# RWKV steps in the order of a list schedule, and experts with eleven weight pieces split ahead and one pinned, in a hybrid layer on one Trainium2 core

## The chip, the cores and the metric

The kernel runs on one core of a Trainium2 chip. The metric is device time in microseconds. Three runs of the kernel before gave 3416.99, 3421.06 and 3427.79 us (median 3421.06). Engines: PE (matmuls), DVE (vector), ACT (scalar), POOL (GpSimd) and SP, which here only issues transfers. Each engine takes its instructions in order; semaphores order the engines against each other.

## The reference, cut to what matters

One layer over 256 context and 2048 latent tokens of width 1024: modulation, one input projection, an mLSTM group and an RWKV-7 group of 8 heads each (64 wide, both scanned forwards and backwards), an output projection with layer norm, then a mixture of 32 SwiGLU experts (two per token) and a last layer norm. What the change touches:

```python
def step(state, inp):                       # RWKV, one token; scanned in two directions
    r_t, w_t, k_t, v_t, kh_t, a_t = inp
    removed = jnp.einsum('zhvk,zhk->zhv', state, kh_t)
    state = (state * w_t[:, :, None, :] - removed[..., None] * (kh_t * a_t)[:, :, None, :]
             + v_t[..., None] * k_t[:, :, None, :])
    return state, jnp.einsum('zhvk,zhk->zhv', state, r_t)

def expert_block(args):                     # 128 tokens of one expert in this kernel
    idx, w, e = args
    xb = tok_pad[idx]
    hb = jax.nn.silu(xb @ ex_gate[e]) * (xb @ ex_up[e])
    return (hb @ ex_down[e]) * w[:, None]
```

## The kernel before, in words

**RWKV stage** (`rwkv`). The 2304 tokens are cut into 9 groups (n) of 256 tokens, a group into 4 chunks of 64 (cc = 2 c2 + c). Both directions (d) go side by side on the halves of the partitions. Per group there is

- *Build*, four times (c2, d). The constructor issues four `pk` loads on SP (L891, 320 KB each, into one of two buffers). `exps` makes decay factors on ACT (L907 to L909), `rows` four DVE products (L917 to L921) that fill KR and BK, `products` 16 small matmuls for each of two chunks (L931) into two PSUM tiles `rpg` and two DVE masks into GM (L935), `turn` a transpose on PE (L940) and a copy on ACT (L941). `rpg` has four buffers.
- *Solve*, once for the group: the 32x32 triangular blocks of GM go through DRAM into `sM` (eight stores `BL` on SP, L963, and two loads, L965), 31 pairs of DVE operations of growing and shrinking size solve them (`steps`, L973 and L975), and `back` brings them home: two stores `YD` (L983), a transposing copy on ACT (L980), two stores `TD` (L985), twelve loads into GM and `T1` (L991, L992). `join(c2)` makes 64x64 inverses out of the blocks: 32 matmuls (L1002), two ACT copies (L1008), 32 matmuls (L1014), two ACT copies (L1019). Its buffers exist once (`sM`, `sY`, `T1`).
- *Chain*, once per chunk, 36 in a row, each needing the state S of the one before: `keys` (PE: 32 matmuls with S, L1046, and 32, L1059; two ACT copies, L1062), `query` (32 matmuls, L1046, latent groups only), `inverse` (32 matmuls, L1071; two ACT copies, L1074), `update` (32 matmuls, L1081), `state` (two DVE operations, L1087 and L1089), `outputs` (32 matmuls, L1097; one ACT copy, L1100; two POOL stores). POOL loads its V rows ahead (L1036).

The order on PE, DVE, ACT and SP is the program's own (`manual_schedule`); POOL's is left to the framework. Before, it is written out by hand: eight Builds and the Solve of group 0 as a prologue, and then a loop over the 36 chunks that puts the Builds of the next two groups (`PLAN`) and pieces of the next group's 31 solve pairs (`CUT`: down to pairs 32, 27, 24 in the first chunk, 23, 17, 15 in the second, and so on) at fixed places between the parts of a Chain. A `state` comes on DVE behind the second piece of its chunk's pairs.

**Experts** (`moe`). The 32 experts follow one another. A weight piece (`split`) is an ACT cast to `eH` (L1531) and a DVE subtraction to `eL` (L1532) of 128x1024 elements; an expert has 12 (4 gate, 4 up, 4 down), in 13 buffers. Eight are split during the expert before (`AHEAD`), pieces 8 and 9 at the expert's start (L1706), and `gate_up` pins the last two with `more(2, m)` (L1609): on DVE they come behind `m`, the first half of the gated product (`mult(0)`, L1622), by an order edge that binds DVE alone; the framework's scheduler places the rest. Behind them on DVE come `aL` (L1553), the low part of the transposed product, and `mult(1)`. Then a branch (L1737) lets further blocks of 128 tokens in, and `tail` multiplies by the down pieces (`epo`, L1565).

Of the kernel before, what the change touches and what calls it, by code (L numbers as in the profile page):

```python
# [8 lines left out]
F = mybir.dt.float32  # L9
# [44 lines left out]
class Kern:  # L54
# [786 lines left out]
    def rwkv(self):  # L841
        tc, nc, s = self.tc, self.nc, self.scratch
        self.Y = s("Y", [2, SEQ, 512])
        with ExitStack() as es:
# [35 lines left out]
            class Build:  # L880
# [3 lines left out]
                def __init__(b, n, c2, d):  # L884
                    b.n, b.c2, b.d, b.g = n, c2, d, grp[d][n]
                    b.lat = b.g > 0
# [24 lines left out]
                def rows(b):  # L911
                    d, v, E, EI = b.d, b.v, Es[b.d], b.v["cu"]
                    b.KR = gp.tile([128, 2, 4, 128], F, name="KR%d" % d)
                    ko, ro = slice(KO[d], KO[d] + 64), slice(RO[d], RO[d] + 64)
# [3 lines left out]
                    nc.vector.tensor_tensor(put(b.BK, ko), b.scan(v["ba"]), b.scan(EI), op=OP.mult)  # L918
                    nc.vector.tensor_tensor(put(b.BK, ro), b.nat(v["km"]), b.nat(EI), op=OP.mult)
# [3 lines left out]
                def products(b, c):  # L923
# [4 lines left out]
                    pG = [pg.tile([128, 4, 128], F, name="rpg") for _ in range(2)]  # L928
                    for q in range(4):
                        for e in range(2):  # L930
                            nc.tensor.matmul(pG[e][:, q, b.cols], b.BK[HD[e], c, q, :], b.KR[HD[e], c, q, b.cols], start=True,  # L931
                                             stop=True, tile_position=(64 * e, 0))
                    m = mask[:, b.d, b.cols][:, None, :].to_broadcast([128, 4, b.cols.stop - b.cols.start])
                    for e in range(2):
                        nc.vector.tensor_tensor(b.GM[:, c, e::2, b.cols], pG[e][:, :, b.cols], m, op=OP.mult)  # L935

                def turn(b, c):
                    pT = pg.tile([128, 4, 128], F, name="rpg")
                    for q in range(4):
                        nc.tensor.transpose(pT[:, q, :], b.BK[:, c, q, :], self.ident)  # L940
                    nc.scalar.copy(b.BT[:, c], pT)  # L941
# [6 lines left out]
            class Solve:  # L948


                def __init__(z, n):
                    z.n, z.j = n, 31
                    z.M = sp.tile([128, 32, 32], F, name="sM")
# [4 lines left out]
                    BLs = [dp.tile([64, 32, 32], F, name="BL%d" % d) for d in range(2)]  # L958
                    for d in range(2):
                        for c2 in range(2):  # L960
                            for i in range(2):
                                b = blk(d, i)
                                nc.sync.dma_start(pr(BLs[d], i, c2), GMf(n, c2, d)[b, :, b])  # L963
                    for d in range(2):
                        nc.sync.dma_start(z.M[64 * d:64 * d + 64], BLs[d])  # L965
# [11 lines left out]
                def back(z):  # L977
                    n, Y = z.n, z.Y
                    YT = sp.tile([128, 32, 32], F, name="sYT")
                    nc.scalar.copy(YT, Y.rearrange("p s t -> p t s"))  # L980
                    YDs, TDs = ([dp.tile([64, 32, 32], F, name="%s%d" % (x, d)) for d in range(2)] for x in ("YD", "TD"))
                    for d in range(2):
                        nc.sync.dma_start(YDs[d], Y[64 * d:64 * d + 64])  # L983
                    for d in range(2):
                        nc.sync.dma_start(TDs[d], YT[64 * d:64 * d + 64])  # L985
# [8 lines left out]
                def join(z, c2):  # L994
                    n, T1 = z.n, z.T1
                    cs = slice(2 * c2, 2 * c2 + 2)
                    Q = pg.tile([128, 16, 32], F, name="rpg")
                    for c in range(2):
                        for h in range(8):
                            for d in range(2):  # L1000
                                lo, hi = blk(d, 0), blk(d, 1)
                                nc.tensor.matmul(Q[hi, 8 * c + h, :], G[n, c2, d][2][lo, c, h, hi], T1[lo, 2 * c2 + c, h, :],  # L1002
                                                 start=True, stop=True, tile_position=(lo.start, hi.start))
                    qs = []
                    for d in range(2):
                        hi = blk(d, 1)
                        qs.append(T1[hi, cs].rearrange("p c h t -> p (c h) t"))
                        nc.scalar.copy(qs[d], Q[hi])  # L1008
                    Q = pg.tile([128, 16, 32], F, name="rpg")
                    for c in range(2):  # L1010
                        for h in range(8):
                            for d in range(2):
                                lo, hi = blk(d, 0), blk(d, 1)
                                nc.tensor.matmul(Q[lo, 8 * c + h, :], qs[d][:, 8 * c + h, :], G[n, c2, d][2][hi, c, h, hi],  # L1014
                                                 start=True, stop=True, tile_position=(hi.start, lo.start))
                    for d in range(2):
                        lo, hi = blk(d, 0), blk(d, 1)
                        src = Q[lo].rearrange("p (c h) t -> p c h t", c=2)
                        nc.scalar.activation(G[n, c2, d][2][lo, :, :, hi], src, AF.Copy, scale=-1.0)  # L1019
# [3 lines left out]
            class Chain:  # L1023
# [31 lines left out]
                def keys(k):  # L1055
                    K = k.K
                    k.from_state(ZKv, K)
                    for q, e, d, h in k.heads():
                        nc.tensor.matmul(ZKv[K[d], e, q, :], k.W[d][2][:, k.c, h, K[d]], k.VZ[d][:, h, :], start=False, stop=False,  # L1059
                                         skip_group_check=True, tile_position=(0, KO[d]))  # L1060
                    for d in range(2):
                        nc.scalar.copy(hv(k.UV[d][K[d]]), ZKv[K[d]])  # L1062
# [5 lines left out]
                def inverse(k):  # L1068
                    K = k.K
                    for q, e, d, h in k.heads():  # L1070
                        nc.tensor.matmul(ZKv[K[d], e, q, :], k.W[d][2][K[d], k.c, h, K[d]], k.UV[d][K[d], h, :], start=True, stop=True,  # L1071
                                         skip_group_check=True, tile_position=(KO[d], KO[d]))
                    for d in range(2):
# [776 lines left out]
```

## Time and profile before

| | us |
|---|---|
| median of three runs (lowest to highest) | 3421.06 (3416.99 to 3427.79) |
| time of the profiled execution | 3418.58 |
| its span | 3417.0 |
| PE, DVE, ACT, POOL busy in the span | 2866.9, 2339.6, 1364.0, 879.0 |
| RWKV stage: first Build's exponentials to last state | 1248.0 to 1944.3 |
| of it, the 36 Chains | 1363.5 to 1944.3 |
| experts: first gate product to last down product | 2306.7 to 3351 |

Times in rows are us from the span's start. A timeline row reads: start, duration, engine, line, operation, out<-in, shape and count, and in brackets the engine's idle time just before it with what ended it. A wait row reads: engine and line that waited, on what; total us, times, longest. A row of the lines view reads: group, count | busy us in total, mean ns of one | idle before it. A windows row reads: stretch and its length; busy us of PE, PEld, DVE, ACT and POOL with their instructions; granted PE clock; share of the DMA engines in use; GB/s.

### The profile page before, as it was taken

How to read it: one execution, taken by the hardware profiler on the slowest of the kernel's cores; microseconds unless marked ns; L12 is line 12 of the kernel's file. 1: busy time of each engine (PE TensorE's matmuls, PEld its weight loads, DVE VectorE, ACT ScalarE, POOL GpSimd, SP SyncE). 2: the span in 40 equal slices, each digit the busy share in tenths (PEclk: the TensorE clock that was granted, in tenths of full speed). 3: DMA queues.
4: the chain of work that ended last, by engine and by line, in shares of the span. 5: the costliest groups of instructions: out<-in, count | busy, mean ns of one | idle time of the engine just before them, and what ended most of it. 6: DMA issues, size and time to landing. Idle time of an engine off the chain costs nothing. (4 is left out here: it accounts for less than half of the span.)

```text
span 3417.0 us, 61401 instructions
## 1 busy us (share of the span) xinstructions
PE 2866.9 (84%) x24042; PEld 2405.9 (70%) x24042; DVE 2339.6 (68%) x3822; ACT 1364.0 (40%) x2187; POOL 879.0 (26%) x862
## 2 busy tenths in 40 slices
PE   6899999999979964777777588859899989989992
PEld 3677788898757754666666567647778877878781
DVE  4488888766787875667656288875877736476447
ACT  4432322335545322334344233344655525355233
POOL 5400000013455660112112365431222212122210
PEclk9899999999979875778788789979999999999996
DMA  5333332235468534666664554448988848597535
GB/s 187 117 114 108 101 116 82 88 101 189 164 219 242 167 109 115 171 159 170 155 168 128 159 174 137 141 147 286 334 295 284 304 125 276 159 335 234 177 112 209
DMA packets 471689, 602.59 MB, mean 176 GB/s; under 512 B 127222, under 2 KB 312338, under 8 KB 471314
## 3 DMA queue, kind: packets, MB, share of 16 engines
q1 hardware_dynamic: 413617, 441.15, 41.2%
q0 software_dynamic: 36736, 129.33, 13.0%
q10 hardware_dynamic: 20960, 27.20, 2.5%
q8 instruction: 224, 3.67, 0.5%
q14 instruction: 152, 1.24, 0.1%
HBM read 453.24 MB, written 144.33 MB: 175 GB/s over the span
## 5 line engine op out<-in xcount | busy, mean ns | idle before, releaser
L1532 DVE TENSOR_TENSOR eL<-eraw,eH 128x1024 fp32r<-128x1024 f32 x384 | 449.6, 1221 | 28.6 <-ACT eH L1531 24.6
L329 DVE SCALAR_TENSOR_TENSOR cacc<-P,cw,cacc 128x1008 f32<-128x1008 f32 (+3 forms) x320 | 398.7, 1247 | 56.5 <-ACT cacc L304 45.6
L1531 ACT CAST eH<-eraw 128x1024 fp32r<-128x1024 f32 x384 | 370.9, 1052 | 48.3 <-PEq L1737 35.1
L263 PE MATMUL in_ps<-hH,w_H 128*128 128x512 f32 (+1 forms) x664 | 252.3, 382 | 1.7 <-ACT pl_ev L355 1.7
L263 PE MATMUL in_ps<-hL,w_H 128*128 128x512 f32 (+1 forms) x664 | 249.6, 377 | 0.0
L263 PE MATMUL in_ps<-hH,w_L 128*128 128x512 f32 (+1 forms) x664 | 248.0, 374 | 0.0
L1565 PE MATMUL epo<-eH,aH 128*128 128x512 f32 x408 | 172.2, 422 | 64.8 <-DVEq L1737 32.2
L1651 POOL DMA_INDIRECT ACC<-yo,ids x32 | 131.0, 4093 | 250.5 <-DVE yo L1650 226.1
L1565 PE MATMUL epo<-eH,aL 128*128 128x512 f32 x408 | 159.7, 404 | 11.7 <-DVE aL L1553 11.7
L1565 PE MATMUL epo<-eL,aH 128*128 128x512 f32 x408 | 163.2, 400 | 0.0
L931 PE MATMUL rpg<-KR,BK 64*128 64x128 f32 (+1 forms) x1152 | 122.4, 350 | 46.7 <-ACT BT L941 17.5
L237 POOL DMA_DIRECT2D w_raw<-in_w_in x28 | 21.2, 757 | 506.2 <-DVE w_L L251 371.8
L263 PEld LDWEIGHTS in_ps<-hH,w_H 128*128 128x128 f32 x664 | 126.2, 191 | 34.6 <-issue 11.5
L931 PEld LDWEIGHTS rpg<-KR,BK 64*128 64x128 f32 x1152 | 104.9, 248 | 63.2 <-issue 23.8
L973 DVE TENSOR_TENSOR sT<-sM,sY 128x31 f32<-128x31 f32 (+15 forms) x279 | 95.3, 342 | 78.8 <-DMA sM<-BL 70.8
L298 ACT COPY P<-in_ps 128x512 f32<-128x512 f32 (+1 forms) x92 | 51.3, 557 | 235.8 <-PE in_ps L263 235.8
L1565 PE MATMUL epu<-eH,xL 128*128 128x256 f32 x512 | 143.4, 283 | 0.0
L1565 PE MATMUL epu<-eL,xH 128*128 128x256 f32 x512 | 143.2, 283 | 0.0
L263 PEld LDWEIGHTS in_ps<-hL,w_H 128*128 128x128 f32 x664 | 126.2, 190 | 22.7 <-issue 2.1
L1565 PE MATMUL epu<-eH,xH 128*128 128x256 f32 x512 | 142.2, 288 | 0.0
L263 PEld LDWEIGHTS in_ps<-hH,w_L 128*128 128x128 f32 x664 | 126.1, 190 | 22.3 <-issue 0.8
L1565 PEld LDWEIGHTS epo<-eH,aH 128*128 128x128 f32 x408 | 78.9, 193 | 83.1 <-ACT xH L1548 30.7
(471 smaller groups left out, 8151.1 us busy)
## 6 DMA issues: line engine op xcount, KB each, us to landing
eraw<-in_ex_gate SPq DMA_DIRECT2D x64, 1024.0 KB
eraw<-in_ex_up SPq DMA_DIRECT2D x64, 1024.0 KB
eraw<-in_ex_down SPq DMA_DIRECT2D x64, 1024.0 KB
pk<-PK SPq DMA_DIRECT2D x144, 320.0 KB
PK<-pk POOLq DMA_DIRECT2D x36, 768.0 KB, 3.9
ada_w<-in_w_ada SPq DMA_DIRECT2D x32, 512.0 KB
v<-MV SPq DMA_DIRECT2D x50, 264.0 KB
kc<-KTd SPq DMA_DIRECT2D x50, 256.0 KB
```

Source lines behind the costliest of these rows:

```text
L237: self.wld = nc.gpsimd.dma_start(w[:, 4:8, o:o + cn], src[:, 4:8])
L263: nc.tensor.matmul(o, a[:, k, :], b, start=i == 0, stop=i == 3 * KT - 1)
L298: nc.scalar.copy(P[:, t0:t0 + n], ps)
L329: nc.vector.scalar_tensor_tensor(o, img[:, r0 + sy:r1 + sy, c0 + sx:c1 + sx], wt(dy, dx), o, op0=OP.mult, op1=OP.add)
L931: nc.tensor.matmul(pG[e][:, q, b.cols], b.BK[HD[e], c, q, :], b.KR[HD[e], c, q, b.cols], start=True, stop=True, tile_position=(64 * e, 0))
L973: nc.vector.tensor_tensor(tt, M[:, 0:j, j:j + 1].to_broadcast([128, j, w]), Y[:, j:j + 1, j:32].to_broadcast([128, j, w]), op=OP.mult)
L1531: self.cp = nc.scalar.copy(H, w)
L1532: nc.vector.tensor_tensor(L, w, H, op=OP.subtract)
L1565: self.pe = nc.tensor.matmul(o, a[:, k, :], b[:, kw, c], start=first and i == 0, stop=last and i == 2)
L1651: nc.gpsimd.indirect_dma_start(out=self.ACC, out_offset=bass.IndirectOffsetOnAxis(ap=cur[:, 0:1], axis=0), in_=y, in_offset=None, compute_ ...
```

## The change

In the RWKV stage the hand-written loop goes. The parts are cut finer (masks apart from products, copies of PSUM apart from the matmuls, `rows` in two halves, the block stores by Build, `join` by half, `keys` with S apart from the rest) and become named steps with an engine, a cost, the steps they come after, a due time and the PSUM tiles they take. A list scheduler places them: of the steps that can start on an engine within 0.4 us of the earliest, the one with the least due time goes first. The chain's steps have due times ahead of everything. The steps are then issued in order of their planned start. No arithmetic is added or removed.

```diff
-            PLAN = [lambda g: [(g + 1, 1, 0), (g + 1, 1, 1)] if g else [], lambda g: [], lambda g: [(g + 2, 0, 0)],
-                    lambda g: [(g + 2, 0, 1)]]
-            CUT = [(32, 27, 24), (23, 17, 15), (13, 9, 8), (1, 1, 1)]
...
+            PER = 13.0
+            DUE = dict(ld=(-92.6, -25.1), rows=(-100.8, -63.4), prod=(-56.5, -92.1), turn=(-47.4, -42.5), solve=-13.0,
+                       join=(1.3, 21.6), look=0.4, step=0.0, blocks=-62.5)
...
+            for i, (n, c2, d) in enumerate(order):
+                key = n, c2, d
+                due = lambda k: 4 * n * PER + DUE[k][c2] + DUE["step"] * d
...
+                step(("ld",) + key, "SP", 0.8, lambda key=key: make(Bs, key, Build, *key), [p("rows2", i - 2), p("ld", i - 1)], due("ld"), 5.0)
+                step(("exps",) + key, "ACT", 1.5, B("exps"), [("ld",) + key, ("rows2",) + order[i - 2] if i > 1 else None, p("exps", i - 1)], due("rows") - 2)
+                step(("rows",) + key, "DVE", 1.35, B("rows"), [("exps",) + key, p("prod", i - 2) and p("prod", i - 2) + (1,),
+                                                            p("turn", i - 2) and p("turn", i - 2) + (1,), p("rows2", i - 1), k("query"), k("keys")], due("rows"))
+                step(("rows2",) + key, "DVE", 1.35, B("more_rows"), [("rows",) + key], due("rows"))
...
+                step(("open", n), "SP", 0.5, Z("open"), bl + ([("back", n - 1), ("transposed", n - 1)] if n else []), due + DUE["blocks"], 2.6)
+                for j in range(31, 0, -1):
+                    nm = ("solve", n, j)
+                    step(nm, "DVE", 2 * (0.165 + 1.05e-3 * j * (32 - j)), Z("steps", j), [last], due + DUE["solve"] - 0.7 * j)
+                    last = nm
+                step(("back", n), "SP", 0.5, Z("back"), [last], due - 13, 2.4)
+                step(("transposed", n), "ACT", 1.95, Z("transposed"), [last, ("back2", n - 1) if n else None], due - 13)
+                step(("back2", n), "SP", 2.4, Z("back2"), [("back", n), ("transposed", n), ("join", n - 1, 1, 1) if n else None,
+                                                         ("joined", n - 1, 1, 1) if n else None], due - 10, 4.0)
...
+                step(("keys", i), "PE", 2.0, K("keys"),
+                     [q("chain", i), ("keys0", i), ("back2", n), ("mask", n, c2, 0, c), ("mask", n, c2, 1, c)], go + 1)
...
+                step(("inv", i), "PE", 1.2, K("inverse"), [("keys_out", i), ("joined", n, c2, 1)], go + 4)
...
+                step(("state", i), "DVE", 1.4, K("state"), [("upd", i)], go + 7)
...
+                        x = min((x for x in c if x[0] <= m + DUE["look"]), key=lambda x: x[1:3])
...
+                for nm in sorted(T, key=lambda x: (start[x], T[x]["at"])):
+                    T[nm]["fn"]()
```

In the experts two numbers change:

```diff
                 m = mult(0)
-                more(2, m)
+                more(1, m)
...
-                W += [split(Rs[e], i) for i in range(len(W), 10)]
+                W += [split(Rs[e], i) for i in range(len(W), 11)]
```

Worked through, the scheduler's rules give this order from one group to the next (here 5 to 6; a number behind a Chain's part is its chunk, and .6.0.1 is n, c2, d):

```text
DVE: solve.5 pairs 11..1, mask.6.0.0 (first), state.19, mask.6.0.0, mask.6.0.1 x2, rows.6.1.0, rows.6.1.1, mask.6.1.0 x2, mask.6.1.1 x2,
     solve.6 pairs 31..26, state.20, pairs 25..19, rows.7.0.0, rows.7.0.1 (state.21 inside it), pairs 18..9, state.22, pairs 8..1
PE:  upd.19, outs.19, prod.6.0.1, keys0.20, prod.6.0.1, turn x4, keys.20, query.20, prod.6.1 x4, join, turn x2, join, turn x2, join, inv.20,
     upd.20, outs.20, join, Chain 21, Chain 22 and 23 with prod.7.0 between
ACT: keys_out.20, exps.7.0.0, join copy, turn copies x2, exps.7.0.1, join copy, turn copies x2, inv copy.20, ...
SP:  back.5, back2.5, blocks.6.0.0, blocks.6.0.1, ld.7.0.0, ld.7.0.1, blocks.6.1.0, blocks.6.1.1, open.6, ld.7.1.0, ld.7.1.1, back.6
```

At the start it puts the Solve of group 0 ahead of the masks of group 1 and of the second pair of group 1's Builds.

## Rows read from the trace of the kernel before

**Rows 1.** Windows view, one stretch of two groups of Chains

```profile
1500.00:1640.00 140.00, 105.26 (x2367) 93.64 (x2362) 92.18 (x204) 56.34 (x98) 27.11 (x52) 0.80 0.66 162
```

**Rows 2.** Waits view, DVE, 1364 to 1862

```profile
DVE sT L973 <- DMA sM<-BL: 70.8, 8, 22.8
DVE KR L917 <- ACT E L907: 54.7, 14, 8.6
```

**Rows 3.** Timeline, SP: solved blocks leave, after Solves 0, 7 and 8

```profile
1349.25 1.13 SPq L983 DMA_DIRECT2D YD<-sY  x2
...
1832.91 1.11 SPq L983 DMA_DIRECT2D YD<-sY  x2
...
1889.56 1.10 SPq L983 DMA_DIRECT2D YD<-sY  x2
```

**Rows 4.** Timeline, DVE: four rows, two masks, a state, the next Solve's first pair

```profile
1536.39 0.68 DVE L917 TENSOR_TENSOR KR<-pk,E 128x512 f32<-128x512 f32 x1
...
1538.79 1.28 DVE L935 TENSOR_TENSOR GM<-rpg,rmask 128x512 f32<-128x512 f32 x2
1539.99 0.40 DVE L973 TENSOR_TENSOR sT<-sM,sY 128x240 f32<-128x240 f32 x1
...
1573.37 0.20 DVE L973 TENSOR_TENSOR sT<-sM,sY 128x31 f32<-128x31 f32 x1 [6.22 <-DMA sM<-BL]
...
1579.29 0.69 DVE L1087 TENSOR_TENSOR ts<-S,rzK 128x512 f32<-128x512 f32 x1 [3.09 <-PE rzK L1081]
```

**Rows 5.** Timeline: group 0's last masks, Solve 0's first and last pair, its blocks back

```profile
1298.48 0.76 DVE L935 TENSOR_TENSOR GM<-rpg,rmask 128x256 f32<-128x256 f32 x2 [2.06 <-PE rpg L931]
...
1325.84 0.20 DVE L973 TENSOR_TENSOR sT<-sM,sY 128x31 f32<-128x31 f32 x1
...
1348.99 0.19 DVE L975 TENSOR_TENSOR sY<-sY,sT 128x31 f32<-128x31 f32 x1
...
1359.66 0.50 SPq L992 DMA_DIRECT2D T<-TD  x1
```

**Rows 6.** Lines view, stage: products, keys' second part, query on PE

```profile
L931 PE MATMUL rpg<-KR,BK 64*128 64x128 f32 (+1 forms) x1152 | 122.4, 350 | 46.7 <-ACT BT L941 17.5 <-DVE BK L919 17.2 <-DVE GM L935 10.9
L1059 PE MATMUL rzK<-VZ,GM 128*64 128x64 f32 x1152 | 69.7, 303 | 0.2
...
L1046 PE MATMUL rzR<-S,KR 64*64 64x64 f32 x1024 | 30.7, 277 | 1.0 <-issue 1.0
```

**Rows 7.** Timeline and waits, SP: sixteen loads, eight block stores, waits of loads

```profile
1271.34 20.82 SPq L891 DMA_DIRECT2D pk<-PK  x16
...
1360.20 5.08 SPq L963 DMA_DIRECT2D BL<-GM  x8
...
SPq L891 <- DVE KR L921: 175.7, 14, 14.4
```

**Rows 8.** Timeline, DVE, states of the last chunks; windows of two of these steps

```profile
1911.91 0.69 DVE L1087 TENSOR_TENSOR ts<-S,rzK 128x512 f32<-128x512 f32 x1 [15.87 <-PE rzK L1081]
1926.06 0.69 DVE L1087 TENSOR_TENSOR ts<-S,rzK 128x512 f32<-128x512 f32 x1 [12.74 <-PE rzK L1081]
1934.35 0.69 DVE L1087 TENSOR_TENSOR ts<-S,rzK 128x512 f32<-128x512 f32 x1 [6.88 <-PE rzK L1081]
...
1911.90:1926.00 14.10, 11.12 (x326) 10.22 (x324) 1.38 (x2) 5.25 (x9) 3.11 (x6) 0.74 0.19 58
1926.00:1943.00 17.00, 12.13 (x398) 11.04 (x395) 2.84 (x5) 5.85 (x10) 3.65 (x10) 0.96 0.68 217
```

**Rows 9.** Timeline of DVE, waits of PE: one expert's gated product, the pieces behind

```profile
2466.97 0.42 DVE L1622 TENSOR_TENSOR act<-act,epu 128x256 f32<-128x256 f32 x1 [1.05 <-PE epu L1565]
2467.31 3.49 DVE L1532 TENSOR_TENSOR eL<-eraw,eH 128x1024 fp32r<-128x1024 f32 x3
...
PE epo L1565 <- DVEq L1737: 32.2, 14, 2.4
...
PE epo L1565 <- DVE aL L1553: 11.7, 12, 1.0
```

More of the change, by code (lines that the diff above doesn't have):

```diff
@@ new lines, in step @@
+            def step(name, eng, us, fn, after=(), due=None, wait=0.0, slots=0, frees=None):
+                T[name] = dict(name=name, eng=eng, us=us, fn=fn, after=[a for a in after if a is not None], due=due, wait=wait,
+                               slots=slots, frees=frees, at=len(T))
+            Bs, Zs, Ks = {}, {}, {}
+            order = [(n, c2, d) for n in range(9) for c2 in range(2) for d in range(2)]
+            PER = 13.0
+            DUE = dict(ld=(-92.6, -25.1), rows=(-100.8, -63.4), prod=(-56.5, -92.1), turn=(-47.4, -42.5), solve=-13.0,
+                       join=(1.3, 21.6), look=0.4, step=0.0, blocks=-62.5)
@@ new lines, in rwkv @@
+            for n in range(9):
+                due = 4 * n * PER
+                Z = lambda m, *a, n=n: (lambda: getattr(Zs[n], m)(*a))
+                bl = []
+                for c2 in range(2):
+                    for d in range(2):
+                        first = not bl
+                        nm = ("blocks", n, c2, d)
+                        step(nm, "SP", 0.5, (lambda n=n, c2=c2, d=d, f=first: (make(Zs, n, Solve, n) if f else None, Zs[n].blocks(c2, d))),
+                             [("mask", n, c2, d, 0), ("mask", n, c2, d, 1), bl[-1] if bl else ("open", n - 1) if n else None], due + DUE["blocks"], 2.2)
+                        bl.append(nm)
+                step(("open", n), "SP", 0.5, Z("open"), bl + ([("back", n - 1), ("transposed", n - 1)] if n else []), due + DUE["blocks"], 2.6)
+                last = ("open", n)
+                for j in range(31, 0, -1):
[6 more added lines that the diff above has]
+                                                         ("joined", n - 1, 1, 1) if n else None], due - 10, 4.0)
+                for c2 in range(2):
+                    for h in range(2):
+                        step(("join", n, c2, h), "PE", 1.2, Z("join", c2, h), [("back2", n) if h == 0 else ("joined", n, c2, 0)],
+                             due + DUE["join"][c2] + 2 * h, 0.0, 1, ("joined", n, c2, h))
+                        step(("joined", n, c2, h), "ACT", 1.2, Z("joined", c2, h), [("join", n, c2, h)], due + DUE["join"][c2] + 1 + 2 * h)
```

245 lines of the change are left out of this document (118 added, 127 removed).

## The prediction, made before the changed kernel ran

> **What bounds the kernel now.** I read the page's slices first, then the windows, the waits by engine, and the timeline of one group. The page's slices show that from the first Build to the last state no engine is full. In the windows [rows 1], two groups of Chains take 140 us with PE busy 105 (at 0.80 of its full clock, so part of it at the low level of 1.2 GHz), DVE 92, ACT 56: a ring of waits, not one engine. The reader should next see how long a group is. The solved blocks leave once per group [rows 3]: from Solve 0 to Solve 7 it is 483.7 us for 7 groups, 69.1 each, and 56.6 for the last, which has no Builds beside it.
>
> Of these 69.1 us DVE works 48. From starts in the timeline [rows 4]: four row products 2.4, a pair of masks 1.2, a state of two operations of 0.69 each 1.4. A Solve without a break takes 23.3 [rows 5]. A group has 4 x 2.4 + 8 x 1.2 + 23.3 + 4 x 1.4 = 48.1. The other 21 us are waits [rows 2]: the trip of the blocks through DRAM (6.2 in [rows 4]), rows that wait for exponentials, which stand on ACT behind copies of the Chain, and the rest in small pieces. A Chain alone is not the bound: where nothing is beside it, states are 8.3 us apart at a granted clock of 0.96, and 14.15 at 0.74 [rows 8], against 69.1 / 4 = 17.3.
>
> The experts are another case: PE is nearly full there, and stands still at one place per expert, ahead of the down products [rows 9].
>
> **The change part by part.** No operation is added in the RWKV stage; it is a new order. So I work out the period P of a group as the new order sets it, with t = 0 where Solve 5's last pair ends.
>
> *From a Solve's end to the next Solve's start.* The blocks come home: the last of the twelve loads was issued, and over, 10.9 us after the YD stores began [rows 3, 5]. `keys.20` waits for all of them, so it starts at t = 10.9. Behind it on PE stand query, then the four products of the group's second pair of Builds. By their sums a keys part is 69.7 / 36 = 1.94, a query 30.7 / 32 = 0.96, a product 122.4 / 72 = 1.70 [rows 6]: products end at 10.9 + 2.9 + 6.8 = 20.6, the last mask at 21.8. DVE's own work in this stretch (one state, two sets of four rows, eight pairs of masks: 1.4 + 4.8 + 9.6 = 15.8) fits under that. Then the trip of 6.2: Solve 6 starts at t = 28.0. On SP, between back2's end at 10.9 and the last blocks, stand two block steps (5.08 / 4 = 1.3 each) and two loads of four transfers. What the loads cost at this place is not shown. Lower bound nothing: they are issued before the last masks end at 21.8. Upper: sixteen transfers took 20.8 us [rows 7], so these eight take 10.4 and, from 13.5 on, fill the queue until 23.9, 2.1 after the last masks. I take nothing, as issuing alone is nearer to the block steps' price, and keep 2.1 for the range.
>
> The Trainium skill ("DMA: Bandwidth & Descriptors", Queues, rings and completion order) says that each DMA engine takes descriptors of one issuer's row in ring order. That speaks against this order, which puts two loads ahead of the last blocks, where the old one put them behind; by it P would be 2.1 longer and the sum 15 us smaller. No row here shows it.
>
> *The Solve's stretch.* DVE has 31 pairs (23.3), three states (4.2) and two sets of rows (4.8): 32.3 if nothing waits. Against before, rows now come after exponentials that ACT does between Chain parts earlier in the group, and masks no longer stand inside. The states stand where they were, behind pairs. Cover for the Chain: the first state began 5.9 us after the Solve's start before [rows 4], so at t = 34; three steps of 8.3 to 11.2 (mean of both clocks) behind it come at 59 to 68, and the next keys may start only at P + 10.9. So P = 28.0 + 32.3 = 60.3 with DVE as the bound, and the Chain just under it.
>
> Bounds of P: with no wait but the trip it is DVE's 15.8 + 6.2 + 32.3 = 54.3; with all the old waits 69.1. I take 60.3, whose terms are each a row.
>
> *Sum over groups.* 7 x (69.1 - 60.3) = 61.6. The last period: 28.0 + 23.3 + 4.2 = 55.5 against 56.6, gain 1.1.
>
> *The start.* Solve 0 began at 1325.8, behind the Builds of group 1; its blocks were masked at 1299.2 [rows 5], and with the trip it could begin at 1305.4, a gain of 20.4. Ahead of it the plan now has two sets of rows that need loads of their own on the same queue, so 17 (bounds 10 and 20.4).
>
> *The end.* Behind Solve 8 there is the same work: blocks home, join, four Chains. Moving the second join ahead of chunk 32's inverse costs a join there and saves one a chunk later: nothing. The output projection waits for the last state as before.
>
> *POOL.* The Chain's loads and the clearing of Y stay there; they are issued at least a step ahead, as before. Nothing.
>
> *Experts.* Behind `mult(0)` DVE does three subtractions, 3.49 us, before `aL` [rows 9], though only two are pinned: the third is there by the scheduler's choice. With one fewer behind, `aL` comes 1.16 earlier, and PE's waits shrink: 14 x 1.16 + 11.7 = 28 us less [rows 9]. With two fewer, DVE needs 2.3 us more ahead of the product, where it has 1.05 of idle time [rows 9]; the product is 1.3 late, and by the worst reading, PE losing that once in each of the 26 places, it costs 34. Unpinning does nothing if the scheduler goes on putting what is left over behind the product. As an unpinned piece stands there now, I take 0; bounds 28 less, 34 more.
>
> *Sum.* 61.6 + 1.1 + 17 = 79.7 off the profiled execution's 3418.6, so 3338.9. The median of the three runs is 2.5 above that execution; I forecast 3341 for the median.
>
> **The rivals.**
>
> *A. The expert pieces move too.* One subtraction leaves the place behind `mult(0)` and the waits of [rows 9] shrink by 28: 3313. For it: in program order pieces 8 to 10 now all come ahead of the product. Against: piece 9 did so before, and is behind it.
>
> *B. The Chain at the low clock sets the period.* With steps of 14.15 [rows 8] the fourth state comes at 34 + 42.5 = 76.5; the next keys could start at P + 10.9, so P = 65.6 and the gain 7 x 3.5 + 18 = 42: 3379. For it: 0.80 now [rows 1]. Against: closer matmuls, as in the last steps at 0.96, went with the high level.
>
> *C. Slower: ACT is held by a load.* `exps.7.0.0` and `exps.7.0.1` now stand on ACT ahead of the join copies and the inverse's copy of the same group's first Chain. Until their loads land, join, inverse, and with them the state, wait, and turn copies that free `rpg` as well. A hold of H beyond t = 26 moves the first state to 34 + H and with three mixed steps of 11.2 gives P = 34 + 33.6 - 10.9 + H = 56.7 + H. Solved against 69.1 + 18.1 / 7 = 71.7, it is slower than before from H = 15. The loads wait on SP for buffers 175.7 / 14 = 12.5 us now [rows 7]; two such waits give H = 25, P = 81.7 and 3421 + 7 x 10 = 3491. Against: by the order their buffers are free at t = 12.
>
> *D. It doesn't do what it says.* Waits that the planner doesn't know put the old pace back; what is gained at the start is lost again: within 10 us of 3421.
>
> **How the numbers follow.** Chances: forecast 0.45, A 0.25, B 0.15, C 0.09, D 0.06. About 0.3%, 10 us, is what a measurement of this kernel can tell from no change. Forecast, A and B are faster by more: 0.85; D 0.06; C 0.09 slower. The range holds the forecast, A and B with their bounds. Its low end is P = 57 (23 less than the forecast) with A's 28: 3290. Its high end is P = 67 and a start worth 17: 3341 + 47 = 3388, taken as 3390. C and D lie outside, and 0.05 at the other end.
>
> **What would show it.** Right: YD stores about 60 us apart, and Solve 0's end near 1332; the last state near 1865; DVE's wait for exponentials nearly gone, its wait for blocks still 6 to 8 per group; in the experts still three subtractions behind `mult(0)`. A: two there, and PE's waits ahead of the down products near 1.2 us. B: granted clock at or under 0.80 in the stage and DVE waiting for PE at states. C: ACT waiting at L907 for pk, longer than 15 us per group. The forecast is wrong if P is under 57 or over 64.

## The result, and the profile after

The changed kernel takes 3361.57 us (median of 4 runs, 3359.01 to 3370.36) against 3422.27 before (4 runs): a ratio of 0.983, 95% interval 0.981 to 0.986, some 60 us less. The forecast was 3341 with a range of 3290 to 3390. The number lies in the range, but it is not made of the forecast's terms. The profiled execution took 3362.69 us, span 3361.1, which is 55.9 less than the span before.

The lines below are of the changed kernel. First the windows view of the stretch of [rows 1]; then the timeline, ACT at the stage's first exponential, SP where the blocks of Solves 0, 7 and 8 leave (as in [rows 3]), DVE at the last state.

```profile
1500.00:1640.00 140.00, 102.13 (x2496) 92.42 (x2494) 92.50 (x209) 58.47 (x103) 27.14 (x52) 0.82 0.64 164
```

```profile
1254.27 0.61 ACT L908 ACTIVATE E<-pk 128x512 f32<-128x512 f32 x1
...
1333.97 1.13 SPq L993 DMA_DIRECT2D YD<-sY  x2
...
1815.85 1.11 SPq L993 DMA_DIRECT2D YD<-sY  x2
...
1867.73 1.72 SPq L993 DMA_DIRECT2D YD<-sY  x2
...
1919.39 0.69 DVE L1106 TENSOR_TENSOR ts<-S,rzK 128x512 f32<-128x512 f32 x1 [7.88 <-PE rzK L1100]
```

The window shows the same picture as before: DVE busy 92 of 140 us, granted clock 0.82 against 0.80. From Solve 0 to Solve 7 it is 481.9 us, 68.8 a group, against 69.1: the period did not move. The RWKV stage, from its first exponential to the last state, took 665.1 us against 694.9 (1942.9 - 1248.0). Of these 29.8 us, 21.5 come at the start (first exponential to the blocks of Solve 0: 79.7 against 101.2), 1.8 from the seven periods, 4.8 from the last period (51.9 against 56.6) and 1.7 behind it. The stage itself was entered 6.2 us later (1254.3 against 1248.0). Nothing ahead of it was changed, and over the runs below its entry lies between 1240.7 (`both`) and 1254.3, so this is no effect of the change. The last period varies as well: it is 55.25 in `rwkv_only`, with the changed order, and 59.55 in `experts_only`, with the old one.

The rest, 32.3 us, comes behind the last state: from the first gate product to the last down product it is 1008.6 us against 1044.7, 36.1 less, and from the last state to the first gate product 3.9 more. Here is the waits view of PE from 2240 to the end, and the timeline of DVE in one expert, as in [rows 9]:

```profile
PE epo L1616 <- PEq L1788: 17.3, 6, 5.0
PE epo L1616 <- ACT eH L1582: 15.8, 13, 1.2
...
PE epo L1616 <- DVEq L1788: 0.8, 1, 0.8
```

```profile
2457.76 0.41 DVE L1673 TENSOR_TENSOR act<-act,epu 128x256 f32<-128x256 f32 x1
2458.09 2.35 DVE L1583 TENSOR_TENSOR eL<-eraw,eH 128x1024 fp32r<-128x1024 f32 x2
2460.36 0.41 DVE L1604 TENSOR_TENSOR aL<-ept,aH 128x256 fp32r<-128x256 f32 x1
```

Two subtractions stand behind `mult(0)` instead of three, and its idle time of 1.05 us is gone: one piece moved ahead of it. PE's wait for DVE at the branch fell from 32.2 us in 14 places to 0.8 in one, and the wait for `aL` is gone. PE's own sequencer at the branch stayed (14.8 before, 17.3 now), and the waits for the cast of a down piece on ACT grew from 7.0 to 15.8, some 1.2 in each of 13 places. Over all causes PE waits ahead of `epo` fell from 76.3 to 45.0 us. That is rival A.

Why did the period stay? The next lines are the waits view, 1364 to 1816, and one group's timeline (Solve 3's blocks leave at 1537.97).

```profile
ACT E L908 <- DMA pk<-PK: 99.1, 17, 11.7
DVE sT L986 <- DMA sM<-BL: 87.5, 7, 15.3
...
DVE ts L1106 <- PE rzK L1100: 35.5, 9, 6.7
```

```profile
1537.97 1.11 SPq L993 DMA_DIRECT2D YD<-sY  x2
...
1551.69 7.88 SPq L892 DMA_DIRECT2D pk<-PK  x8
1559.67 3.44 SPq L969 DMA_DIRECT2D BL<-GM  x4
1564.83 1.90 SPq L978 DMA_DIRECT2D sM<-BL  x2
...
1552.42 4.87 DVE L943 TENSOR_TENSOR GM<-rpg,rmask 128x512 f32<-128x512 f32 x8 [3.57 <-PE rpg L937]
...
1569.72 0.20 DVE L986 TENSOR_TENSOR sT<-sM,sY 128x31 f32<-128x31 f32 x1 [12.43 <-DMA sM<-BL]
...
1559.99 0.63 ACT L908 ACTIVATE E<-pk 128x512 f32<-128x512 f32 x1 [8.59 <-DMA pk<-PK]
...
1592.07 0.63 ACT L908 ACTIVATE E<-pk 128x512 f32<-128x512 f32 x1 [5.95 <-DVE sT L986]
...
1600.02 0.69 DVE L1106 TENSOR_TENSOR ts<-S,rzK 128x512 f32<-128x512 f32 x1 [4.39 <-PE rzK L1100]
```

Two things are to be seen. First, the last masks end at 1557.3, but the blocks of that pair leave only at 1559.7 to 1563.1, when the eight loads have gone, and DVE waits 12.4 us for its Solve instead of the 6.2 of [rows 4]. Secondly, ACT stands 6 us at the exponential of `exps.5.1.0` at 1592, whose loads were issued at 1583.2, as soon as the rows had freed the buffer. (The row puts this wait down to a DVE pair that ended just before; of the 17.5 us a group that ACT waits at exponentials, 15.4 are put down to the load itself.) Behind it on ACT is the keys copy of the third Chain, so the third state comes 15.8 us after the second, and DVE, which has its remaining pairs queued behind that state, waits 4.4. DVE no longer waits for exponentials itself, as forecast; ACT does, and through it the Chain.

The period stayed, but its two parts did not. These are the blocks of Solves 3 and 4 of the kernel before, on SP:

```profile
1549.69 1.11 SPq L983 DMA_DIRECT2D YD<-sY  x2
...
1618.21 1.11 SPq L983 DMA_DIRECT2D YD<-sY  x2
```

With its first pair at 1573.37 [rows 4], Solve 4 began 23.7 us after the blocks of Solve 3 left, and its stretch, up to its own blocks, took 44.8. Over the seven groups the means are 24.8 and 44.3; in the changed kernel they are 31.8 and 37.0. So the new order did shorten the Solve's stretch, by 7.3, and lost 7.0 ahead of it.

### The profile page after: what moved, and what is told of

It is laid out like the page before. It is cut to its first block, busy times and chain, and to the rows that moved or that the text cites. A ratio compares the mean times of both kernels' runs of the same rounds, so it can differ in the third digit from the quotient of the medians.

```text
span 3361.1 us, 61457 instructions
## 1 busy us (share of the span) xinstructions
PE 2828.1 (84%) x24042; PEld 2381.4 (71%) x24042; DVE 2340.2 (70%) x3822; ACT 1363.1 (41%) x2187; POOL 926.2 (28%) x862
## 5 line engine op out<-in xcount | busy, mean ns | idle before, releaser
L1583 DVE TENSOR_TENSOR eL<-eraw,eH 128x1024 fp32r<-128x1024 f32 x384 | 449.3, 1219 | 33.9 <-ACT eH L1582 33.2
L1702 POOL DMA_INDIRECT ACC<-yo,ids x32 | 175.3, 5477 | 240.0 <-DVE yo L1701 217.2
L1616 PE MATMUL epo<-eH,aH 128*128 128x512 f32 x408 | 170.8, 419 | 44.4 <-PEq L1788 17.3
L937 PE MATMUL rpg<-KR,BK 64*128 64x128 f32 (+1 forms) x1152 | 99.2, 315 | 65.2 <-DVE GM L943 41.9
L937 PEld LDWEIGHTS rpg<-KR,BK 64*128 64x128 f32 x1152 | 87.5, 219 | 74.3 <-DVE GM L943 42.7
L1052 POOL DMA_DIRECT2D UV<-RVT x72 | 37.3, 521 | 338.9 <-PE rzR L1116 261.0
```

Of the source, the lines that this page charges most:

```text
L1052: nc.gpsimd.dma_start(x[k.R[d]].rearrange("p h v -> p (h v)"), self.RVT[k.t0[d]:k.t0[d] + 64, :])
L1583: nc.vector.tensor_tensor(L, w, H, op=OP.subtract)
L1616: self.pe = nc.tensor.matmul(o, a[:, k, :], b[:, kw, c], start=first and i == 0, stop=last and i == 2)
L1702: nc.gpsimd.indirect_dma_start(out=self.ACC, out_offset=bass.IndirectOffsetOnAxis(ap=cur[:, 0:1], axis=0), in_=y, in_offset=None, compute_ ...
```

## The experiments

The table sums each profile from Solve 0's blocks to Solve 7's, divided by 7: the period, DVE's wait ahead of a Solve's first pair for its blocks, DVE's waits ahead of states, ACT's waits ahead of the first exponential of a Build. Ratios are to the kernel before, run beside each, with their 95% intervals. The 9.1 in the first row is one wait of 22.8 us, behind Solve 0 [rows 2], and six of 6.1 to 8.4.

| kernel | median us | ratio | period | blocks | states | ACT at exps |
|---|---|---|---|---|---|---|
| before | 3422.27 | | 69.1 | 9.1 | 1.5 | 0 |
| changed | 3361.57 | 0.983 (0.981 to 0.986) | 68.8 | 12.5 | 5.1 | 17.5 |
| rwkv_only | 3399.00 | 0.993 (0.991 to 0.996) | 69.0 | 12.5 | 5.3 | 17.3 |
| experts_only | 3386.22 | 0.989 (0.987 to 0.991) | 69.1 | 9.5 | 1.2 | 0 |
| exps_behind | 3326.84 | 0.973 (0.971 to 0.975) | 64.6 | 12.7 | 1.5 | 15.4 |
| loads_behind | 3289.14 | 0.960 (0.959 to 0.962) | 60.7 | 7.0 | 2.7 | 8.1 |
| both | 3302.08 | 0.966 (0.964 to 0.969) | 60.2 | 6.8 | 3.8 | 8.6 |
| late_second | 3287.55 | 0.963 (0.960 to 0.966) | 59.2 | 6.8 | 2.6 | 5.0 |
| prices | 3334.47 | 0.975 (0.972 to 0.978) | 66.0 | 0.2 | 15.2 | 6.3 |
| prices_both | 3295.09 | 0.963 (0.960 to 0.966) | 59.7 | 0 | 10.0 | 1.4 |
| loads_pool | 3350.32 | 0.980 (0.978 to 0.983) | 68.2 | 11.9 | 5.0 | 15.4 |
| half_behind | 3349.55 | 0.979 (0.975 to 0.983) | 67.6 | 8.5 | 7.2 | 15.7 |
| half_late | 3322.05 | 0.972 (0.968 to 0.976) | 63.9 | 9.8 | 5.3 | 15.1 |
| twelve | 3421.23 | 1.000 (0.998 to 1.001) | | | | |

Each diff below is against the changed kernel unless it says otherwise.

**The two parts alone.** The RWKV order with the experts of before:

```diff
-                more(1, m)
+                more(2, m)
...
-                W += [split(Rs[e], i) for i in range(len(W), 11)]
+                W += [split(Rs[e], i) for i in range(len(W), 10)]
```

> The changed RWKV order with the experts as before (two pieces pinned, ten ahead). Theory (the parts add up, and the period of a group hardly moved): the trace of the changed kernel has its last state 23.5 us earlier than before (1919.4 against 1942.9), so 3422 - 23.5 = 3399, ratio 0.993, and PE's waits ahead of the down products are the old 76 us. Rival (the forecast's split, 80 us from the RWKV stage and none from the experts): all of the 60 us, 3362.

And the kernel before with the same two lines turned the other way:

> The RWKV stage as before, one piece pinned and eleven ahead. Theory (the experts gave the larger part): PE's waits ahead of the down products fall from 76 to 45 us as they did in the changed kernel, so 3422 - 31 = 3391, ratio 0.991, with two subtractions behind the first half of the gated product instead of three. Rival (the forecast: the scheduler leaves three pieces there): 3422 within 10 us.

Measured 3399.0 and 3386.2, 0.67% and 1.09% less, together 1.76% where the change has 1.69%. The parts add up, and the experts, which the forecast had at nothing, give the larger one. The forecast's split falls. The 3399 of the theory was met more closely than its terms, though: in the profiled execution of `rwkv_only` the last state comes 32.5 us earlier than before instead of 23.5, and what follows takes 13.5 longer with the same code.

**The loads behind the blocks.** One more thing that the first pair's loads come after, and the plan is made anew:

```diff
-                step(("ld",) + key, ..., [p("rows2", i - 2), p("ld", i - 1)], due("ld"), 5.0)
+                step(("ld",) + key, ..., [p("rows2", i - 2), p("ld", i - 1), ("open", n - 1) if n > 1 and c2 == 0 else None], due("ld"), 5.0)
```

> In the changed kernel the two pk loads of the next group's first pair also wait until the blocks of this group are read back. Theory (SP's order costs the trip): the Solve's wait for its blocks goes from 12.4 back to 6 to 7 us, it starts some 6 us sooner behind the Solve before, and as the join copies no longer stand behind an exponential that waits for a load, the Chain follows. The period goes from 68.8 to about 63: 7 x 6 = 42 less, 3362 - 42 = 3320. Rival (the Chain sets the period, the wait only moves): DVE waits some 6 us longer per group at the states, the period stays above 67, time within 12 us of 3362.

Measured 3289.1: more than the theory asked, and the rival falls. The timeline (DVE, one Solve's first pair, the first two states behind it) and the window of [rows 1]:

```profile
1532.52 0.21 DVE L986 TENSOR_TENSOR sT<-sM,sY 128x31 f32<-128x31 f32 x1 [6.69 <-DMA sM<-BL]
...
1534.59 0.68 DVE L1106 TENSOR_TENSOR ts<-S,rzK 128x512 f32<-128x512 f32 x1
...
1548.05 0.69 DVE L1106 TENSOR_TENSOR ts<-S,rzK 128x512 f32<-128x512 f32 x1 [2.67 <-PE rzK L1100]
```

```profile
1500.00:1640.00 140.00, 108.50 (x2720) 96.89 (x2718) 108.09 (x241) 64.36 (x111) 34.21 (x66) 0.90 0.76 187
```

The wait for blocks is 7.0, as it was before the change in all groups but the first. The edit also moved the exponentials of the first pair behind the join copies on ACT, and ACT's waits ahead of exponentials halved, 17.5 to 8.1, and with them the waits at states. So this run alone took two things away. The period, 60.7, is near the forecast's 60.3, but it is 26.2 + 34.5 where the forecast had 28.0 + 32.3.

**The exponentials behind the third Chain step.** Only the second pair's exponentials get a later place:

```diff
-                step(("exps",) + key, ..., [..., p("exps", i - 1)], due("rows") - 2)
+                step(("exps",) + key, ..., [..., p("exps", i - 1), ("inv_out", 4 * n - 6) if n > 1 and c2 else None], due("rows") - 2)
```

> In the changed kernel the exponentials of the next group's second pair also wait until the inverse's copy of the third Chain is done. Theory (ACT's order holds the third Chain step: the exponential waits 6.0 us for its load ahead of the keys copy, and DVE then 4.4 us at the third state): this wait of DVE goes, the period falls by 4.4 to about 64.4, 7 x 4.4 = 31 less, 3331. Rival (the third state is late by the low clock of PE, not by ACT): DVE still waits over 3 us there, time within 10 us of 3362.

Measured 3326.8, period 64.6. The waits view, 1364 to 1775:

```profile
ACT E L908 <- DMA pk<-PK: 77.4, 20, 9.8
DVE sT L986 <- DMA sM<-BL: 74.7, 6, 14.1
...
DVE ts L1106 <- PE rzK L1100: 10.6, 6, 2.8
```

DVE's wait at states falls from 35.5 to 10.6, while the wait for blocks stays. ACT waits nearly as long at exponentials as before (15.4 against 17.5), only in a place where less hangs on it. The theory stands.

**Both, and one of two.** `both` has the loads behind and puts the exponentials of the first pair behind the second Chain's inverse copy, those of the second pair behind the third's; `late_second` leaves the first pair's where the plan puts them.

> Loads behind the read-back of the blocks, and the exponentials of both pairs behind the inverse's copies of the second and the third Chain. Theory (each wait is its own term of the period): what is left in the run with the loads behind, 2.7 us of DVE at the second state and 1 to 2 elsewhere in the Solve, goes too; the period falls from 60.7 to about 58, 7 x 2.5 = 18 less: 3271. Rival (DVE's own work and the trip are the bound once the loads are behind): within 8 us of the 3289 of that run.

> The run with the loads behind, and of the exponentials only the second pair kept behind the third Chain's inverse copy. Theory (what the run with both lost, it lost by the first pair's exponentials, whose rows then came behind the second state): the period is a little under the 60.7 of the loads behind alone, 7 x 1 less than 3289: 3282. Rival (ACT's order has nothing left to give once the loads are behind): 3289 or more, up to the 3302 of both.

`both` took 3302.1, neither the 3271 of the theory nor within 8 of 3289; its period, 60.2, is half a microsecond under that of the loads alone. ACT waits 8.6 us at exponentials instead of 8.1, and DVE 3.8 at states instead of 2.7, now mostly at the fourth state of a group. So the two holds do not add up. The rival's reason, that the trip and DVE's own work are the bound, is nearer but not shown: DVE is busy 45.5 of the 60.2 and waits 6.8 for blocks, and the other 7.9 are waits at states (3.8), for products (1.9) and in small pieces. `late_second` has the shortest period, 59.2, and 3287.6 us, which can't be told from the loads alone: its theory's gain of 7 is too small to see. These two beat both kernels, the changed one by 2.2%. Why `both` is 13 us above `loads_behind` in the medians, where their profiled executions agree (3296.8 and 3298.6), stays open.

**The prices in the plan.** The planner's costs for SP set to what the trace shows:

```diff
-                step(("ld",) + key, "SP", 0.8, ..., due("ld"), 5.0)
+                step(("ld",) + key, "SP", 4.0, ..., due("ld"), 4.3)
...
-                        step(nm, "SP", 0.5, ..., due + DUE["blocks"], 2.2)
+                        step(nm, "SP", 1.2, ..., due + DUE["blocks"], 2.0)
...
-                step(("open", n), "SP", 0.5, ..., due + DUE["blocks"], 2.6)
+                step(("open", n), "SP", 1.9, ..., due + DUE["blocks"], 3.0)
...
-                step(("back", n), "SP", 0.5, Z("back"), [last], due - 13, 2.4)
+                step(("back", n), "SP", 1.1, Z("back"), [last], due - 13, 1.8)
...
-                step(("back2", n), "SP", 2.4, ..., due - 10, 4.0)
+                step(("back2", n), "SP", 9.5, ..., due - 10, 0.0)
```

> The changed kernel with the costs that its trace shows for SP's steps in the plan: a load step 4.0 us instead of 0.8, a pair of block stores 1.2 instead of 0.5, the read-back 1.9 instead of 0.5, blocks home 9.5 instead of 2.4. By the plan one of the two loads now goes behind the last blocks, and the exponential goes behind the third keys copy. Theory (the plan went wrong by SP's prices): the trip is about 9 us, half of the lost time, and the hold at the third step shrinks; the period is about 63, 7 x 6 = 42 less than 3362: 3320. Rival (a list that issues whatever can start puts a load ahead of the blocks in any case): over 3350.

> The same prices, and loads and exponentials kept behind as in the run with both. Theory (once the two orders are fixed the prices have little left to do): within 10 us of the run with both, 3271. Rival (the plan's other choices still suffer from the wrong prices): 3255 or less.

Prices alone took 3334.5, between theory and rival. The waits view of DVE, 1364 to 1800, shows where the time went:

```profile
DVE ts L1106 <- PE rzK L1100: 92.9, 13, 15.4
...
DVE sT L986 <- DMA sM<-BL: 1.6, 3, 0.9
```

The plan now puts the group's first state ahead of the Solve's first pair, and ACT still has an exponential, with its load, ahead of the second join copy. The wait for blocks did not shrink; DVE stands through it at the state instead (in the group behind Solve 3 the first pair starts 31.6 us after the Solve before, against 31.75, and even behind that state it waits 0.45 for its blocks). With the two orders fixed by hand and the same prices, `prices_both` took 3295.1, between the runs with `both` and `late_second`, off the theory's 3271 by more than its 10 us and far from the rival's 3255. It is within 7 us of `both` as measured, so the theory's reason, that the prices have little left to do, holds; its number came from the missed theory of `both`. Right costs gave 27 us, the rule that says what must not come first 72.

**SP's issuing, or the DMA engines?** The eight loads take SP 7.88 us to issue, and 2.62 MB to move. To tell these apart, POOL issues the first pair's loads, at the same place of the plan:

```diff
-                        nc.sync.dma_start(b.pk[:, q], ...)
+                        (nc.gpsimd if n > 1 and c2 == 0 else nc.sync).dma_start(b.pk[:, q], ...)
```

> The changed kernel, its plan and its orders as they are; only the pk loads of the first pair of a group are issued by POOL instead of SP. Theory (the blocks wait for SP, which takes 7.9 us to issue these eight loads): with SP free the blocks leave as the masks end, and DVE's wait for them goes from 12.4 to 7 or 8 us; the hold of the third step stays. The period falls by 4 to 5, 3362 - 7 x 4.5 = 3330. Rival (the loads' data stands ahead of the blocks in the DMA engines, whoever issues it): the wait stays over 11 us and the time within 10 us of 3362.

Measured 3350.3, period 68.2, wait for blocks 11.9: by the wait the rival, whose time is missed by a little (11 us under 3362, where it allowed 10). The timeline of that run (POOL's loads, the last masks, the block stores and the read-back on SP, the Solve), and windows of it; the two windows of the changed kernel stand behind for comparison, loads and then blocks:

```profile
1537.82 3.48 POOL L892 DMA_DIRECT2D pk<-PK  x4 [1.01 <-DVE KR L927]
...
1542.41 3.47 POOL L892 DMA_DIRECT2D pk<-PK  x4
...
1545.48 3.68 DVE L943 TENSOR_TENSOR GM<-rpg,rmask 128x512 f32<-128x512 f32 x6 [0.23 <-PE rpg L937]
...
1540.33 14.16 SPq L969 DMA_DIRECT2D BL<-GM  x8
1554.88 1.62 SPq L978 DMA_DIRECT2D sM<-BL  x2
...
1560.20 0.21 DVE L986 TENSOR_TENSOR sT<-sM,sY 128x31 f32<-128x31 f32 x1 [11.04 <-DMA sM<-BL]
```

```profile
1537.80:1546.00 8.20, 7.09 (x107) 6.88 (x109) 3.94 (x7) 1.16 (x2) 8.05 (x10) 0.58 1.08 254
1546.00:1549.20 3.20, 3.09 (x89) 2.73 (x87) 3.16 (x6) 1.17 (x3) 0.00 (x0) 1.00 1.08 268
1549.20:1554.50 5.30, 4.45 (x144) 3.85 (x143) 0.00 (x0) 3.37 (x8) 0.00 (x0) 1.00 0.89 205
```

```profile
1551.70:1559.70 8.00, 6.42 (x134) 5.56 (x130) 4.87 (x8) 0.00 (x0) 0.00 (x0) 1.00 0.99 269
1559.70:1563.10 3.40, 0.77 (x20) 0.64 (x22) 0.00 (x0) 3.00 (x7) 0.00 (x0) 0.77 1.09 279
```

The last masks end at 1549.2, no load stands ahead of the blocks on SP, the loads even left 8.8 us after the Solve before instead of 13.7, and still the stores are issued only by 1554.5. In both kernels the DMA engines are full while the loads run (share 0.99 to 1.09) at 254 to 279 GB/s; from 1549.2 to 1554.5 the share is 0.89. The DMA view tells the queues apart (packets, MB, share of the 16 engines). First `loads_pool`, 1547 to 1550, POOL's queue and SP's; then the changed kernel, 1554 to 1562, where both loads and stores are on SP's:

```profile
q0 software_dynamic: 234, 0.79, 98.9%
q1 hardware_dynamic: 104, 0.01, 3.0%
```

```profile
DMA packets 4683, 2.33 MB, mean 291 GB/s; under 512 B 152, under 2 KB 4683, under 8 KB 4683
```

In these 3 us of POOL's loads SP's queue gets 3.0% of the DMA engines, with block stores issued on it. So what holds the blocks is mostly the bytes of the loads, and not the place that issues them. SP's issuing is not free of it: its eight stores spread over 14.2 us here, waits for masks included, and the last two alone take 5.0, where all eight took 5.1 in [rows 7]; what that adds was not separated. If it is the bytes, half of them should be through in time:

```diff
-  ("open", n - 1) if n > 1 and c2 == 0 else None
+  ("open", n - 1) if n > 1 and c2 == 0 and d else None
```

(against `loads_behind`; `half_late` has the same edit against `late_second`).

> As the run with the loads behind, but only one of the two loads of the first pair is kept behind the read-back; the other stays ahead of the last blocks, as in the changed kernel. Theory (the bytes of the loads fill the DMA engines, at the 270 GB/s that the windows show): one load of 1.31 MB takes 4.9 us from 13.7 after the Solve's end and is through at 18.6, before the last masks end at 19.3, so DVE's wait for the blocks is 6.7 to 8 us; the period is 61 to 62 and the time near the 3289 of that run, 3285 to 3298. Rival (a load ahead of the blocks costs its place, whatever its size, through SP and through the exponential that ACT holds ahead of the join copy): the wait is over 9 us and the time over 3312.

> As the run with one load behind, and the second pair's exponentials behind the third Chain's inverse copy. Theory (with the trip whole and ACT not held at the third step, the rows of the next group come a little earlier than in the run with late_second): 3287 within 6. Rival (the hold at the join copy comes back with the load ahead): over 3300.

The first half of the theory holds in part, and the time does not. In `half_behind` the wait for blocks is 8.5 on average (10.3 and 11.7 in the first two groups, 6.7 to 8.5 in the others), where the theory had 6.7 to 8 and the rival over 9. In `half_late` it is 9.8, which is the rival's. The bytes still tell where the wait is long. In the first two groups of `half_behind` the last masks end 15.9 and 17.0 us after the Solve before, ahead of the time when a load issued at 13.0 and 14.0 can be through; in five groups of `half_late` the load leaves only at 15.8 to 17.0, and the masks end at 18.8 to 20.2. An estimate from these rows, 7.0 for the trip plus what is left of the load's 4.9 us when the last masks end, gives 7.6 and 8.6 for the two runs, some 1 us short of both. The time of `half_behind` is 3349.6, as the rival had it, and mostly by the second of the rival's two reasons. With one load ahead, the plan puts its exponential back ahead of the join copy on ACT, and the second pair's ahead of the third keys copy. One group of it, ACT and then DVE:

```profile
1548.79 0.63 ACT L908 ACTIVATE E<-pk 128x512 f32<-128x512 f32 x1 [8.27 <-DMA pk<-PK]
1550.20 1.18 ACT L1032 COPY T<-rpg 32x512 f32<-32x512 f32 x2
...
1577.67 0.63 ACT L908 ACTIVATE E<-pk 128x512 f32<-128x512 f32 x1 [7.70 <-DVE sT L986]
```

```profile
1558.82 0.69 DVE L1106 TENSOR_TENSOR ts<-S,rzK 128x512 f32<-128x512 f32 x1 [2.51 <-PE rzK L1100]
...
1585.62 0.69 DVE L1106 TENSOR_TENSOR ts<-S,rzK 128x512 f32<-128x512 f32 x1 [5.05 <-PE rzK L1100]
```

What the Solve gains at its start it gives back at the first and the third state, and the period is 67.6. `half_late` takes the second hold away, and the period falls to 63.9, by 3.7 where `exps_behind` had 4.2. Its 3322 us miss the theory's 3287 and are on the rival's side, over 3300. Against `late_second`, with the same exponentials late, one load ahead costs 4.7 us of period: DVE waits 3.0 more at the blocks and 2.7 more at the states, and a little less elsewhere.

**No piece pinned.** The other end of the experts' edit:

```diff
-                more(1, m)
+                more(0, m)
...
-                W += [split(Rs[e], i) for i in range(len(W), 11)]
+                W += [split(Rs[e], i) for i in range(len(W), 12)]
```

> The changed kernel with all twelve pieces split ahead and none pinned. Theory (DVE's idle time ahead of the first half product is used up, 0 to 0.4 us of it are left where there were 1.05; PE's wait of 1.2 us ahead of the down products is for the cast of a down piece on ACT, which this edit does not move earlier): a subtraction of 1.16 more ahead makes the product about 0.8 late in each of 32 experts, at worst 26 us more: 3362 to 3388. Rival (the piece behind the product is still what PE waits for): a further 1.2 less in the 13 experts that wait, 3346.

Measured 3421.2, 60 above the changed kernel: the direction of the theory, beyond its worst reading of 26. The timeline of DVE in one expert, and the waits view of PE from 2240 to the end:

```profile
2466.88 6.89 DVE L1583 TENSOR_TENSOR eL<-eraw,eH 128x1024 fp32r<-128x1024 f32 x6
2473.69 0.41 DVE L1673 TENSOR_TENSOR act<-act,epu 128x256 f32<-128x256 f32 x1
2475.04 0.42 DVE L1604 TENSOR_TENSOR aL<-ept,aH 128x256 fp32r<-128x256 f32 x1 [0.94 <-ACT aH L1599]
```

```profile
PE ept L1591 <- DVE act L1673: 54.0, 31, 1.8
...
PE epx L1591 <- DVE xL L1604: 16.6, 29, 0.7
```

Two pieces moved ahead at once, the pinned one and the one that the scheduler had left, so the product is late by up to 1.8 us in 31 places (54.0 us), and the transposes of the next tokens wait 9.6 more (16.6 against 7.0). The waits for casts are gone in exchange (15.8). These three make 48 of the 63 us between the two spans; the rest was not traced. Three, two and no pieces behind the product thus stand at 3399, 3362 and 3421 with the same RWKV order. One piece was not tried.

## Why the prediction was right in its number and wrong in its parts

*The period, 61.6 us of the forecast's 79.7.* It gave 1.8. Two steps failed.

The first is "I take nothing" for the two loads ahead of the last blocks, with 2.1 as the upper bound. The upper case itself was nearly exact: issued from 13.5 on, full until 23.9; measured 13.7 and 25.1 (the end of the last store at 1563.1). But the bound was a difference of two times, and the other one moved: four products took 4.9 us instead of 6.8 (the granted clock from 1551.7 to 1559.7 is 1.00, the level of 2.4 GHz), and the masks ended at 19.3 instead of 21.8. So the loads, not the masks, set the Solve's start, 31.75 instead of 28.0. The price row to take was [rows 7], the sixteen transfers, not the block steps. The sentence on the Trainium skill ("DMA: Bandwidth & Descriptors", Queues, rings and completion order) pointed the right way, and the trace agrees: with both on SP's row, the blocks came behind the loads (152 of 4683 packets from 1554 to 1562 are under 512 B). That it is not the ring alone is shown by `loads_pool`. The same section of the Trainium skill says that a DMA engine alternates packet by packet between the rows that have work. By that the blocks on SP's row should pass between the packets of POOL's. Some did, 104 packets of SP's row beside 234 of POOL's, but with 0.01 MB against 0.79, and the wait is 11.9 instead of 12.5; whether the turns were strict the view does not show.

The second is "32.3 if nothing waits" in the Solve's stretch. Measured 36.7; the difference is the 4.39 at the third state. Rival C had the mechanism, ACT held at an exponential by its load, and put it at the first pair's exponentials and the first Chain step. There H was at most 1.6 us (the first state at 35.6 after the Solve's end instead of 34), and DVE waited only 0.28 for it, at 1573.60: the state stands behind six pairs of a Solve that itself began 3.75 late. Where the Solve begins sooner, in `half_behind`, the same hold shows as 2.5 at the first state. The larger hold was at the second pair's exponential and the third step: its load cannot leave before the rows of the first pair free the buffer, inside the Solve, and it took 8.9 us to come. C's sign, over 15 us of ACT waits a group, was there (17.5); most of it hid beside other work, so the period was the old one and not a longer one.

28.0 + 32.3 became 31.75 + 36.7 = 68.5, by chance nearly the old 69.1, which was 24.8 + 44.3. The forecast never took the old period apart like this; its own 28.0 was already later than the old start. Taking the loads away gave 60.7, late exponentials with it 59.2: P was near the period of an order that the change did not yet have, with terms that differ from the forecast's (26.2 + 34.5 and 25.9 + 33.2), so part of that nearness is luck too.

*The start, 17.* Measured 21.5, just above the upper bound of 20.4. The two sets of rows ahead of Solve 0 cost nothing that shows there.

*The last period, 1.1.* Measured 4.8, and 1.7 behind it. With the same order `rwkv_only` has 1.4 in place of the 4.8, so most of this may be the spread between executions.

*The experts, 0.* This was the step "as an unpinned piece stands there now, I take 0". The trace of before had one piece behind the product that nothing pinned, and the forecast took this for the place where any further piece would go. It was one left-over piece: with one pin fewer two stand there, and with none pinned, none. Rival A, with its 28, measured 31.3 in PE's waits. Its terms were 16.2 at the branch and 11.7 for `aL`; measured were 31.4 and 11.7, less 8.8 that came back as waits for casts and 2.5 at PE's sequencer, so its total is nearer than its terms. The signs named for it, two subtractions and waits near 1.2 us, are both there.

*B* did not come about: the clock stayed at 0.82, and the states that waited did so for ACT. With the loads behind it was 0.90. *D* was half right: unknown waits did put the old pace back, but the gain at the start was kept.

So the range held because two errors of opposite sign met: 59.8 us too much in the period, 31.3 too little in the experts, and 9.9 too little at start and end. The forecast's 79.7 with these corrections is 61.1; less the later entry of 6.2, and with 1.0 behind the experts' waits, it is the 55.9 between the two spans.

## What to carry to other kernels

A list scheduler issues whatever can start; a transfer that can start but is not needed yet takes the DMA engines from a small one that is. Give each critical trip a rule about which large loads may not go before it. On an engine that works in order, ask of each instruction that waits for a load what stands behind it, in every stage of the round, and not only in the first. And where a change has two parts, price each against its own rival: here their errors cancelled, and only the parts alone showed it.

## What the runs showed of the hardware

Loads of 2.62 MB and the block stores beside them filled all DMA engines for 11.4 us (8.0 + 3.4 and 8.2 + 3.2 in the windows above) at 254 to 279 GB/s, and the blocks came about as late when another engine issued the loads (11.9 against 12.5 us). In that run a queue of small stores got 3.0% of the DMA engines beside one of large loads with 98.9% (1547 to 1550). Without loads ahead of it the same trip takes 6.8 to 7.0. The entry into a stage can differ by 13.6 us between executions with the same code ahead of it (1240.7 to 1254.3), so the start of a stage is to be read from its own first instruction and not from the start of the span.
